# Tie order of a top-k selection and the place of the sample rows' retention, in a one-layer hybrid decoder step

## The chip, the cores and the metric

One core of a Trainium2 chip runs the whole kernel as one program. The metric is the device time of one execution in microseconds; lower is better. Times of several executions are compared by their median.

## What is computed

One decoder layer for a prompt of 1024 tokens and for 8 sample rows with a past of 2048 tokens each, on shared weights:

```python
x = LN1(alpha*x + 0.5*SwiGLU_1(x))
h = x @ w_in                      # q,k,v of attention; indexer q,k,w; q,k,v,gate of retention
# attention, 8 heads x 64: an indexer scores all causal keys,
I[t,s] = sum_h w[t,h] * relu(q_idx[t,h] . k_idx[s])
# lax.top_k keeps 256 keys per query (ties: the lowest index first); softmax over those with a bias
# retention, 4 heads x 128: per chunk, o = (q k^T * decay) v + (q S) * decay ; S = g*S + k^T v
#   sample rows: one step, S_new = gamma_h * S + k v^T ; o = q S_new ; group norm, swish gate
x = LN2(alpha*x + concat(A, R) @ w_out)
x = LN3(alpha*x + 0.5*SwiGLU_2(x))
```

The outputs are y for prompt and samples, the new k, v and indexer-key rows, and the retention states. The 8 sample states are 4 x 128 x 128 floats each (256 KB), read and written once.

## The kernel before

**Layout.** Activations lie transposed, in three column chunks of 344 tokens (`CW`, together 1032). A projection tile of 128 output columns is three calls of `dense` (line 169 to 171: 24 matmuls of 128x344 into one PSUM bank of kind `mm`), followed by an evacuation per chunk (`ev`) on ScalarE and VectorE. PSUM has 8 banks; in the stage in question (`MB`, line 1947) they are `mm=[0,1]`, `sc=[3,4]`, `po=[2,5]`, `aux=[6,7]`; each kind rotates over its banks, so the third chunk of a run of tiles waits until the first one's bank is evacuated.

**The planner.** The work is written as Python generators driven by `Sched`. Each generator emits some instructions and yields a delay in planner microseconds; the main line emits a half tile of matmuls and ticks the planner clock by 1.75, and due generators emit between. `drain` and `until` tick by 0.25 until a generator has ended or a condition holds. So the planner fixes the program order. The framework then orders each engine's own queue at build time, mostly in program order, but it lets a later instruction pass one that it expects to be held up. On the chip each queue runs strictly in its order.

**The stage in question.** In program order after the gate tile of the last retention head:

- `topk` (line 1010) has searched each query row's 256th largest score bit by bit. Its tail (lines 1063 to 1079) settles ties: for each key block b it counts scores at or over the threshold (`ge`, line 1068), marks equal ones (`eq`, 1069), scans them (`pf`, 1070), works out how many to drop (`need`, 1072 and 1073), and builds the mask `M[b]` (1075 and 1076 on VectorE, 1077 on ScalarE). Block b has (b+1)*128 columns. The order is b = 2 to 7, with yields of 2.5 and 2.0. `done.add(b)` lets the attention use that block.
- `ret_core(3)` finishes the last prompt retention head (matmuls `rs`, `ro`, `pyt`; VectorE lines 1156 to 1215).
- `sret` (line 1221) does the sample rows' retention: it loads two states, then per sample b broadcasts the value row on TensorE (`spread`, line 1100, into an `sc` bank), scales the state on ScalarE (1254, four instructions), multiplies and adds on VectorE (1255, 1256), stores the state from the SP queue (1258), multiplies it with q into a `po` bank that is kept for all eight samples (1260, eight instructions), and loads the state for b+2 (1263). A norm, four transposes (1277) and a store of 16 KB (1281) end it. Its yields per sample are `sr_step` = 3.0 and 1.0. It is started right behind the last gate tile.
- The main line emits the tiles va0, qa0, ka0 (attention values, queries and keys of head pair 0), drains `topk` between qa0 and ka0, and then starts `att_lane`, which runs 8 units per head pair: logits into `sc`, mask and bias on VectorE, exponential on ScalarE, transposes into `aux`, products with the values into a `po` bank. `g.po_free` counts free `po` banks. The units of the first three pairs begin with the largest query blocks (6 and 7).
- Under pair 0's attention it emits va1 and qa1 with a pace of 2.0, drains `sret`, and goes on with ka1. So it goes on to pair 3, the output projection and the second SwiGLU.

Of the kernel before, what the change touches and what calls it, by code (L numbers as in the profile page):

```python
# [15 lines left out]
F32 = mybir.dt.float32  # L16
# [10 lines left out]
P = 128  # L27
D = 1024
NTOK = 1032
CW = 344  # L30
# [55 lines left out]
def bank(g, kind, name):  # L86

    ks = g.banks[kind]
    t = g.ps.tile([P, 512], F32, tag=f"b{ks[g.bi[kind] % len(ks)]}", name=name, bufs=1)
    g.bi[kind] += 1  # L90
    return t
# [6 lines left out]
def A(g, slot, name, dt=F32, n=NTOK):  # L98

    return g.ap.tile([P, n], dt, tag=f"a{slot}", name=name, bufs=1)  # L100
# [909 lines left out]
def topk(g, S, M, tk, hi, lo, scr, tie, done):  # L1010


    nc = g.nc
    V = nc.vector
    bl = ACTB + DVEB
    na = len(ACTB)
    lim, cn = tk['c'][:, 0:6], tk['c'][:, 6:12]
    cnt, t, t2, c, lim2, T1 = (tk[k] for k in ('cnt', 't', 't2', 'cond', 'lim2', 'T1'))
    for j, b in enumerate(bl):
        n = (b + 1) * 128  # L1020
        sortkey(g, S[b], n, scr[0], scr[1], hi[b], lo[b])
        yield 2.5
    g.keysdone = True
    key = hi
    for ph in range(2):
        V.memset(t, -0.5 if ph == 0 else 32767.5)
        L = lim if ph == 0 else lim2

        def count(nm):
            for j, b in enumerate(bl):  # L1030
                n = (b + 1) * 128
                if j < na:
                    jk = g.ms.tile([P, 1024], BF, tag="ja", name=f"ja{nm}{b}", bufs=1)
                    nc.scalar.activation(jk[:, 0:n], key[b], AF.Sign, bias=t[:, j:j + 1], scale=-1.0, accum_out=cnt[:, j:j + 1])  # L1034
                else:
                    jk = g.ms.tile([P, 640], BF, tag="jv", name=f"jv{nm}{b}", bufs=1)
                    V.tensor_scalar(out=jk[:, 0:n], in0=key[b], scalar1=t[:, j:j + 1], scalar2=None, op0=OP.is_lt, op1=OP.add, accum_out=cnt[:, j:j + 1])

        count(f"{ph}x")
        for bit in range(15, -1, -1):  # L1040
            step = 2.0 ** bit
            nc.gpsimd.tensor_scalar(out=t2, in0=t, scalar1=0.5 * step, scalar2=None, op0=OP.subtract)
            yield g.tk_step
            V.tensor_tensor(out=c, in0=cnt, in1=L, op=OP.is_le)
            V.scalar_tensor_tensor(out=t, in0=c, scalar=step, in1=t2, op0=OP.mult, op1=OP.add)  # L1045
            if bit:
                count(f"{ph}_{bit}")

        if ph == 0:
            V.tensor_copy(T1, t)  # L1050
            V.tensor_scalar(out=t, in0=t, scalar1=0.5, scalar2=None, op0=OP.add)
            count("g")
            for j, b in enumerate(bl):
                V.scalar_tensor_tensor(out=lo[b], in0=hi[b], scalar=T1[:, j:j + 1], in1=lo[b], op0=OP.is_equal, op1=OP.mult)
                if j % 2:
                    yield 2.0
            V.tensor_tensor(out=lim2, in0=lim, in1=cn, op=OP.add)
            V.tensor_tensor(out=lim2, in0=lim2, in1=cnt, op=OP.subtract)
            key = lo
    th = tk['th']  # L1060
    threshold_bits(g, T1, t, tk['i0'], tk['i1'], th)
    ge, eq, pf = tie()
    for b in (2, 3, 4, 5, 6, 7):
        j = bl.index(b)
        n = (b + 1) * 128
        thj = th.bitcast(F32)[:, j:j + 1]
        need = g.ms.tile([P, 1], F32, tag="need", name=f"need{b}", bufs=2)
        V.tensor_scalar(out=ge[:, 0:n], in0=S[b], scalar1=thj, scalar2=None, op0=OP.is_ge, op1=OP.add, accum_out=cnt[:, j:j + 1])
        V.tensor_scalar(out=eq[:, 0:n], in0=S[b], scalar1=thj, scalar2=None, op0=OP.is_equal)
        V.tensor_tensor_scan(out=pf[:, 0:n], data0=eq[:, 0:n], data1=eq[:, 0:n], initial=0.0, op0=OP.add, op1=OP.bypass)  # L1070

        V.tensor_scalar(out=need, in0=cnt[:, j:j + 1], scalar1=-1.0, scalar2=256.0, op0=OP.mult, op1=OP.add)
        V.tensor_tensor(out=need, in0=need, in1=pf[:, n - 1:n], op=OP.add)
        yield 2.5
        V.scalar_tensor_tensor(out=eq[:, 0:n], in0=pf[:, 0:n], scalar=need, in1=eq[:, 0:n], op0=OP.is_gt, op1=OP.mult)
        V.tensor_tensor(out=ge[:, 0:n], in0=ge[:, 0:n], in1=eq[:, 0:n], op=OP.subtract)
        nc.scalar.activation(M[b], ge[:, 0:n], AF.Identity, bias=g.nbig[:, 0:1], scale=BIG)
        done.add(b)
        yield 2.0


class Rows:
# [135 lines left out]
    nc.sync.dma_start(mscr[hd, :, 0:1024], gT[:, 0:1024])  # L1218


def sret(g, smp, state_ret, state_out, mscr, sa, sb):

    nc = g.nc
    V = nc.vector
# [2 lines left out]
    ks = cv(32).rearrange("p (h b) -> p h b", h=4)  # L1227
    qm = cv(256).rearrange("p (h b) -> p h b", h=4)
    kv = cv(512).rearrange("p (h v) -> p h v", h=4)
    vn = Rows(g, [g.ms.tile([40, CW], F32R, tag="silu", name=f"srr{j}", bufs=2)[:, 0:256] for j in range(2)])  # L1230
    mix = cv(32).rearrange("p (h b) -> p h b", h=4)
    st = cv(24, rows=8).rearrange("p (h b) -> p h b", h=4)
    mv = cv(8, rows=8).rearrange("p (h b) -> p h b", h=4)
# [8 lines left out]
    for b in range(2):  # L1242
        nc.sync.dma_start(s2[b], state_ret[b].rearrange("h d v -> d h v"))
    yield 3.0
    while not g.po_free:
        yield 0.5
    g.po_free -= 1
    po = bank(g, 'po', "sro")
    for b in range(8):
        s0 = s2[b % 2]  # L1250
        pv = bank(g, 'sc', f"srv{b}")
# [13 lines left out]
    o = s2[0][0:8]  # L1265
    nc.scalar.copy(o, po[0:8].rearrange("p (h v) -> p h v", h=4))
    g.po_free += 1
    for h in range(4):
        V.bn_stats(out=st[:, h, :], in_=o[:, h, :])
        V.bn_aggr(out=mv[:, h, :], in_=st[:, h, :])  # L1270
# [679 lines left out]
def trunk(tc, i, o):  # L1950
# [156 lines left out]
    for c in range(NCH):  # L2107
# [3 lines left out]
        if c == 2:  # L2111
            S_.close("msL")
            zt = [X(g, f"z{q}", f"zt{q}") for q in range(3)]
            M, S = {}, {}
            mt = zt[0][:, 0:2304].bitcast(BF)
            for b in range(8):
                M[b] = mt[:, b * (b + 1) // 2 * 128:(b + 1) * (b + 2) // 2 * 128]
            cz = Carve(zt[0], 8 * CW)
            cz(2304)
            sbias = cz(128).rearrange("p (c h) -> p c h", c=16)  # L2120
            for k in ('qaT', 'kaT', 'vaT', 'q', 'k', 'g', 'v'):
                smp[k] = cz(32).rearrange("p (a b) -> p a b", a=4)
            g.kvd = cz(4)
            g.wsmp = cz(8, rows=8)
            g.ptab = cz(1, I32)
            sel = dict(np64=cz(2, rows=64), row=cz(16, I32), bkt=cz(16, I32), bias=sbias, rel_bias=i['rel_bias'])
            cz = Carve(zt[1], 8 * CW)
            for b in (7, 6, 5):
                S[b] = cz((b + 1) * 128)
            cz = Carve(zt[2], 8 * CW)  # L2130
            for b in (4, 3, 2):
                S[b] = cz((b + 1) * 128)
            sx = cz(130)[:, 0:129]
            _, g.coff, _ = pack()
            g.csts = cz(i['csts'].shape[1])
            g.qis = cz(32).rearrange("p (a b) -> p a b", a=4)
            g.stats = [(cz(48).rearrange("p (a b) -> p a b", a=8), cz(16).rearrange("p (a b) -> p a b", a=8), cz(8)) for _ in range(2)]
            tk = dict(c=cz(12))
            for k in ('cnt', 't', 't2', 'cond', 'lim2', 'T1'):
                tk[k] = cz(6)  # L2140
            for k in ('i0', 'i1', 'th'):
                tk[k] = cz(6, I32)
            nc.sync.dma_start(g.csts, i['csts'])
            nc.sync.dma_start(tk['c'], i['tkc'])
            nc.sync.dma_start(g.kvd, i['kvd'])
            g.ms = S_("msI")
            cm = g.ms.tile([P, 256], F32, name="cmask")
            nc.sync.dma_start(cm, i['cmask'])
            g.cmask = cm[:, 0:128]
            nc.vector.tensor_copy(M[0], cm[:, 128:256])  # L2150
            nc.vector.memset(M[1][:, 0:128], 0.0)
            nc.vector.tensor_copy(M[1][:, 128:256], cm[:, 128:256])
# [81 lines left out]
    g.tk_step, g.s2_step, g.s3_step = 3.2, 2.5, (4.0, 2.0)  # L2234

    def tie_tiles():
        t = A(g, 16, "tie").bitcast(BF)
        return t[:, 0:1024], t[:, 1024:2048], A(g, 17, "tief")

    tks = s.add(topk(g, S, M, tk, hi, lo, (u, sk), tie_tiles, g.mdone))  # L2240
    sm = Carve(g.ms.tile([P, 988], F32, tag="s1", name="s1sm", bufs=1), 988)
# [1 line left out]
    for hd in (1, 2, 3):  # L2243
# [8 lines left out]
        t = A(g, 6, f"gT{hd}")  # L2252
        tile(ev_copy(g, t, smp['g'][:, hd, :], AF.Silu), f"gr{hd}")
        gT[hd] = t
    sr = s.add(sret(g, smp, i['state_ret'][0], o['ret_state_sample'][0], mscr, A(g, 20, "sra"), A(g, 21, "srb")))


    kout = o['k_prompt'][0, 0].rearrange("t h d -> t (h d)")
# [19 lines left out]
    s.drain(*cores)  # L2278
    nat = s.add(after())
    tile(pair_q(g, 0, pr[0], smp, A(g, 9, "q00", F32R, 1024), A(g, 1, "q10", F32R, 1024))[0], "qa0")  # L2280
    s.drain(tks, nat)
    g.z2 = zt[2]
    nat = s.add(keys(0, g.z2[:, 0:1024], 0.0)())
    s.drain(nat)
    S_.close("msR")
    g.ms = S_("msA")
    g.nt_tag = "nt"
    qz = X(g, "z1", "qx", F32R)
    qx = qz[:, 0:2048]
    g.low = [(0, g.ms.tile([P, 512], F32R, name="klA")), (320, qz[:, 2048:2752])]  # L2290
    pr[0].ready = True
    lane = s.add(att_lane(g, pr, M, ascr))
    s.tick(0)
    for ct in (1, 2, 3):
        s.drain(nat)
        after = values(ct, g.z2[:, 0:1024], g.att_pace)
        s.until(lambda: ct == 1 or pr[ct - 2].done())
        nat = s.add(after())
# [265 lines left out]
```

## Time and profile before

| | us |
|---|---|
| median of 3 runs | 2315.74 |
| lowest and highest of them | 2314.35 and 2316.15 |
| the profiled execution's own time | 2317.26 |
| its span in the trace | 2315.5 |
| TensorE busy | 2223.6 |
| VectorE busy | 1760.2 |
| ScalarE busy | 1071.5 |

The span covers all but 1.8 us of the profiled execution's time. Busy times are sums over the span and hide where an engine waits; the stage in question lies at 1106 to 1215 us.

### The profile page before, as it was taken

How to read it: one execution, taken by the hardware profiler on the slowest of the kernel's cores; microseconds unless marked ns; L12 is line 12 of the kernel's file. 1: busy time of each engine (PE TensorE's matmuls, PEld its weight loads, DVE VectorE, ACT ScalarE, POOL GpSimd, SP SyncE). 2: the span in 40 equal slices, each digit the busy share in tenths (PEclk: the TensorE clock that was granted, in tenths of full speed). 3: DMA queues.
4: the chain of work that ended last, by engine and by line, in shares of the span. 5: the costliest groups of instructions: out<-in, count | busy, mean ns of one | idle time of the engine just before them, and what ended most of it. 6: DMA issues, size and time to landing. Idle time of an engine off the chain costs nothing.

```text
span 2315.5 us, 36887 instructions
## 1 busy us (share of the span) xinstructions
PE 2223.6 (96%) x14155; PEld 2147.5 (93%) x14155; DVE 1760.2 (76%) x3745; ACT 1071.5 (46%) x1931; POOL 326.1 (14%) x342
## 2 busy tenths in 40 slices
PE   8999999999999999899899999889999999999996
PEld 8999999999999998888789889879799999999996
DVE  5755797887878588777966678988468789887876
ACT  5433343342434466887456664353445444343331
POOL 0000100000002303454023224313210000000002
PEclk9999999999999999999899999989999999999998
DMA  8544332222222201222222142436544332222311
GB/s 266 153 138 146 108 90 74 83 76 64 82 78 96 92 23 46 57 74 58 85 72 56 44 148 71 130 119 191 168 136 137 93 109 80 92 73 64 92 65 49
DMA packets 239182, 224.32 MB, mean 97 GB/s; under 512 B 13098, under 2 KB 219774, under 8 KB 238238
## 3 DMA queue, kind: packets, MB, share of 16 engines
q1 hardware_dynamic: 235166, 209.38, 29.9%
q0 software_dynamic: 3840, 12.59, 1.7%
q8 instruction: 111, 1.82, 0.3%
q14 instruction: 65, 0.53, 0.1%
HBM read 200.91 MB, written 22.59 MB: 97 GB/s over the span
## 4 chain that ended last, share of the span: by engine, by line
PE 76%; DVE 11%; ACT 7%; issue 3%; DMA 2%; POOL 1%; SPq 0%; POOLq 0%; DVEq 0%; ACTq 0%
PE pds_f L403 5%; PE pds_f L404 5%; PE pds_f L405 5%; ACT ja L1034 3%; PE pg_f L169 2%; PE pg_f L170 2%; PE pu_f L169 2%; PE pdp_f L403 2%; PE pg_f L171 2%; PE pdp_f L404 2%; PE pdp_f L405 2%; PE pu_f L171 2%; PE pu_f L170 2%; PE ps_f1U L169 2%; PE ps_f2G L170 2%
## 5 line engine op out<-in xcount | busy, mean ns | idle before, releaser
L407 DVE SCALAR_TENSOR_TENSOR z<-pds_f,z 128x344 f32<-128x344 f32 x320 | 164.7, 516 | 126.4 <-PE pds_f L405 125.1
L403 PE MATMUL pds_f<-gs_f,wh_f1ds 128*128 128x344 f32 x352 | 114.3, 325 | 0.1
L407 DVE SCALAR_TENSOR_TENSOR z<-pdp_f,z 128x344 f32<-128x344 f32 x160 | 80.0, 512 | 44.1 <-PE pdp_f L405 43.9
L405 PE MATMUL pds_f<-gs_f,wl_f1ds 128*128 128x344 f32 x352 | 113.5, 322 | 0.0
L403 PE MATMUL pds_f<-gs_f,wh_f2ds 128*128 128x344 f32 x352 | 113.4, 322 | 0.0
L404 PE MATMUL pds_f<-gs_f,wh_f1ds 128*128 128x344 f32 x352 | 113.4, 322 | 0.0
L405 PE MATMUL pds_f<-gs_f,wl_f2ds 128*128 128x344 f32 x352 | 112.4, 319 | 0.0
L404 PE MATMUL pds_f<-gs_f,wh_f2ds 128*128 128x344 f32 x352 | 112.4, 319 | 0.0
L1034 ACT ACTIVATE ja<-key,zt 128x1024 bf16<-128x1024 int16 (+5 forms) x90 | 93.8, 1042 | 37.3 <-DVE zt L1045 30.2
L723 POOL TENSOR_TENSOR yt<-yt,ln_b_rows 128x512 f32<-128x512 f32 (+1 forms) x9 | 12.0, 1351 | 570.3 <-ACT yt L722 570.3
L296 ACT CAST wS_f1G<-ws_f1G 128x512 fp32r<-128x512 f32 x44 | 25.0, 618 | 133.4 <-PE pds_f L404 68.1
L1508 ACT CAST p<-pT 128x512 fp32r<-128x512 f32 (+2 forms) x112 | 47.5, 434 | 54.2 <-PE pT L1504 42.0
L296 ACT CAST wS_f2G<-ws_f2G 128x512 fp32r<-128x512 f32 x44 | 25.7, 619 | 93.4 <-PE pds_f L405 80.7
L403 PEld LDWEIGHTS pds_f<-gs_f,wh_f1ds 128*128 128x128 f32 x352 | 66.9, 190 | 1.0 <-DVE z L407 0.3
L404 PEld LDWEIGHTS pds_f<-gs_f,wh_f1ds 128*128 128x128 f32 x352 | 67.0, 190 | 0.2
L405 PEld LDWEIGHTS pds_f<-gs_f,wl_f1ds 128*128 128x128 f32 x352 | 66.8, 190 | 0.0
L403 PEld LDWEIGHTS pds_f<-gs_f,wh_f2ds 128*128 128x128 f32 x352 | 66.2, 188 | 0.2 <-ACT gs_f L465 0.2
L404 PEld LDWEIGHTS pds_f<-gs_f,wh_f2ds 128*128 128x128 f32 x352 | 66.2, 188 | 0.0
L405 PEld LDWEIGHTS pds_f<-gs_f,wl_f2ds 128*128 128x128 f32 x352 | 66.1, 188 | 0.0
L612 POOL TENSOR_TENSOR lns_l<-z 128x344 f32<-128x344 f32 x3 | 2.8, 938 | 442.2 <-DVE z L407 428.0
L1509 DVE TENSOR_TENSOR p<-pT,p 128x512 fp32r<-128x512 f32 (+2 forms) x112 | 54.5, 497 | 8.7 <-ACT p L1508 7.5
L169 PE MATMUL pg_f<-xh,wh_f1g 128*128 128x344 f32 x176 | 57.5, 326 | 2.8 <-ACT xh L762 2.8
(815 smaller groups left out, 8651.8 us busy)
## 6 DMA issues: line engine op xcount, KB each, us to landing
wr_f1g<-in_ffn_wg_dram SPq DMA_DIRECT2D x22, 512.0 KB
wr_f1u<-in_ffn_wu_dram SPq DMA_DIRECT2D x22, 512.0 KB
wr_f1dp<-in_ffn_wd_dram SPq DMA_DIRECT2D x22, 512.0 KB
wr_f1G<-in_ffn_wg_dram SPq DMA_DIRECT2D x22, 512.0 KB
wr_f1U<-in_ffn_wu_dram SPq DMA_DIRECT2D x22, 512.0 KB
wr_f1ds<-in_ffn_wd_dram SPq DMA_DIRECT2D x22, 512.0 KB
wr_f2u<-in_ffn_wu_dram SPq DMA_DIRECT2D x22, 512.0 KB
wr_f2g<-in_ffn_wg_dram SPq DMA_DIRECT2D x22, 512.0 KB
```

The lines of the kernel that those rows point to most:

```text
L169: g.nc.tensor.matmul(ps, w[0][:, k, :], x[0][:, k, :], start=first and i == 0, stop=False)
L170: g.nc.tensor.matmul(ps, w[0][:, k, :], x[1][:, k, :], start=False, stop=False)
L171: g.nc.tensor.matmul(ps, w[1][:, k, :], x[0][:, k, :], start=False, stop=last and i == n - 1)
L296: nc.scalar.copy(t[:, 0], src)
L403: g.nc.tensor.matmul(ps, wh[:, o, :], th, start=i == 0, stop=False)
L404: g.nc.tensor.matmul(ps, wh[:, o, :], tl, start=False, stop=False)
L405: g.nc.tensor.matmul(ps, wl[:, o, :], th, start=False, stop=i == len(grp) - 1)
L407: g.nc.vector.scalar_tensor_tensor(out=z, in0=ps, scalar=0.5 / ALPHA, in1=z, op0=OP.mult, op1=OP.add)
L723: nc.gpsimd.tensor_tensor(out=y[0:n, sl], in0=y[0:n, sl], in1=gb['ln3_b'][0:n, sl], op=OP.add)
L1034: nc.scalar.activation(jk[:, 0:n], key[b], AF.Sign, bias=t[:, j:j + 1], scale=-1.0, accum_out=cnt[:, j:j + 1])
L1508: nc.scalar.copy(ph[:, js, ts], ptv[:, js, ts])
L1509: nc.vector.tensor_tensor(out=pl[:, js, ts], in0=ptv[:, js, ts], in1=ph[:, js, ts].bitcast(F32), op=OP.subtract)
```

## The change

It reverses the order in which ties are settled (b = 7 first), and lets the generator yield 3.0 and 3.5 instead of 2.5 and 2.0. The tie tiles lie in slots 14 and 15 instead of 16 and 17, `need` lies in a long-lived tile. The main line waits before ka0 only until blocks 6 and 7 are settled, and for the rest of `topk` at the start of pair 1's tiles. ka0's transposed keys lie in `zt[1]` instead of `zt[2]`. `sret` starts when `topk` and `ret_core(3)` have ended; it takes bank 5 for its sum, leaves bank 2 as the only `po` bank until that sum is read, and has one row tile of 512 columns instead of two of 256.

```diff
-    for b in (2, 3, 4, 5, 6, 7):
+    for b in (7, 6, 5, 4, 3, 2):
...
-        need = g.ms.tile([P, 1], F32, tag="need", name=f"need{b}", bufs=2)
+        need = tk['need'][:, b % 2:b % 2 + 1]
...
-        yield 2.5
+        yield 3.0
...
-        yield 2.0
+        yield 3.5
...
-def sret(g, smp, state_ret, state_out, mscr, sa, sb):
+def sret(g, smp, state_ret, state_out, mscr, sa, sb, rows):
...
-    vn = Rows(g, [g.ms.tile([40, CW], F32R, tag="silu", name=f"srr{j}", bufs=2)[:, 0:256] for j in range(2)])
+    vn = Rows(g, [rows])
...
-    while not g.po_free:
-        yield 0.5
-    g.po_free -= 1
-    po = bank(g, 'po', "sro")
+    while g.po_free < 2:
+        yield 0.25
+    g.po_free = 1
+    g.banks['sr'], g.bi['sr'], g.banks['po'] = [5], 0, [2]
+    po = bank(g, 'sr', "sro")
...
     g.po_free += 1
+    g.banks['po'] = [2, 5]
...
+            tk['need'] = cz(2)
...
-        t = A(g, 16, "tie").bitcast(BF)
-        return t[:, 0:1024], t[:, 1024:2048], A(g, 17, "tief")
+        t = A(g, 14, "tie").bitcast(BF)
+        return t[:, 0:1024], t[:, 1024:2048], A(g, 15, "tief")
...
-    sr = s.add(sret(g, smp, i['state_ret'][0], o['ret_state_sample'][0], mscr, A(g, 20, "sra"), A(g, 21, "srb")))
+    sr = s.add(later(lambda: not s.live(tks) and not any(s.live(e) for e in cores), lambda: sret(
+        g, smp, i['state_ret'][0], o['ret_state_sample'][0], mscr, A(g, 20, "sra"), A(g, 21, "srb"), A(g, 7, "srr", F32R)[0:40, 0:512])))
...
-    s.drain(tks, nat)
+    s.drain(nat)
+    s.until(lambda: {6, 7} <= g.mdone)
     g.z2 = zt[2]
-    nat = s.add(keys(0, g.z2[:, 0:1024], 0.0)())
+    nat = s.add(keys(0, zt[1][:, 0:1024], 0.0)())
...
-    qz = X(g, "z1", "qx", F32R)
-    qx = qz[:, 0:2048]
-    g.low = [(0, g.ms.tile([P, 512], F32R, name="klA")), (320, qz[:, 2048:2752])]
...
         s.drain(nat)
+        if ct == 1:
+            s.drain(tks)
+            qz = X(g, "z1", "qx", F32R)
+            qx = qz[:, 0:2048]
+            g.low = [(0, g.ms.tile([P, 512], F32R, name="klA")), (320, qz[:, 2048:2752])]
```

## Rows read from the trace of the kernel before

**Rows 1.** The page, part 1: busy us (share of the span) xinstructions.
```profile
PE 2223.6 (96%) x14155; PEld 2147.5 (93%) x14155; DVE 1760.2 (76%) x3745; ACT 1071.5 (46%) x1931; POOL 326.1 (14%) x342
```

**Rows 2.** Busy time by stretch: va0 to ka0, then va1 and qa1.
```profile
core 0: us, PE busy (x) PEld busy (x) DVE busy (x) ACT busy (x) POOL busy (x), PEclk, DMA share, GB/s
1105.85:1179.22 73.37, 63.04 (x365) 55.22 (x365) 62.86 (x138) 29.59 (x74) 8.92 (x5) 0.88 0.32 91
...
1179.22:1214.99 35.77, 33.59 (x220) 31.61 (x219) 22.06 (x80) 18.82 (x43) 8.62 (x11) 1.00 0.26 68
```

**Rows 3.** Timeline of TensorE: start us, us, instruction, count, idle before and its releaser.
```profile
1118.16 0.76 PE L1100 MATMUL srv<-srr,sel 40*128 40x256 f32 x2 [3.64 <-DVE need L1072]
...
1134.81 0.79 PE L1100 MATMUL srv<-srr,sel 40*128 40x256 f32 x2 [2.93 <-DVE srb L1255]
...
1161.05 0.39 PE L169 MATMUL pw_ka<-h1h,wh_ka 128*128 128x344 f32 x1 [3.76 <-DVE q L1418]
```

**Rows 4.** Timeline of TensorE: a projection matmul behind the first wait, one behind the third.
```profile
1119.30 0.49 PE L170 MATMUL pw_va<-h1l,wh_va 128*128 128x344 f32 x1
...
1161.28 0.32 PE L170 MATMUL pw_ka<-h1l,wh_ka 128*128 128x344 f32 x1
```

**Rows 5.** Timeline of VectorE: the instructions that ended the three waits, and one scan.
```profile
1117.75 0.26 DVE L1181 SCALAR_TENSOR_TENSOR kd<-kd,rs 128x128 f32<-128x128 f32 x1
...
1134.07 0.68 DVE L1255 TENSOR_TENSOR srb<-srv,srb 128x512 f32<-128x512 f32 x1
...
1155.20 2.28 DVE L1070 TENSOR_TENSOR_SCAN tief<-tie 128x1024 f32<-128x1024 bf16 x1
...
1160.39 0.52 DVE L1418 SCALAR_TENSOR_TENSOR q<-pw_qa,q 64x344 fp32r<-64x344 f32 x1
```

**Rows 6.** Groups of VectorE, 1105.85 to 1179.22: xcount | busy us, mean ns | idle before.
```profile
L1070 DVE TENSOR_TENSOR_SCAN tief<-tie 128x384 f32<-128x384 bf16 (+5 forms) x6 | 9.7, 1620 | 0.1
L1075 DVE SCALAR_TENSOR_TENSOR tie<-tief,need,tie 128x384 bf16<-128x384 f32 (+5 forms) x6 | 5.7, 950 | 0.1
L1255 DVE TENSOR_TENSOR srb<-srv,srb 128x512 f32<-128x512 f32 x8 | 5.5, 685 | 0.1
L1256 DVE TENSOR_TENSOR sra<-sra,srb 128x512 f32<-128x512 f32 x8 | 5.5, 683 | 0.1
...
L1403 DVE TENSOR_TENSOR kk<-pw_ka,k 64x344 fp32r<-64x344 f32 x4 | 2.1, 519 | 2.0 <-ACT k L1400 1.9
...
L1215 DVE SCALAR_TENSOR_TENSOR gT<-pyt,prm,gT 128x512 f32<-128x512 f32 x2 | 1.5, 752 | 2.2 <-PE pyt L1212 2.2
...
L1096 DVE TENSOR_TENSOR srr<-srvn,srr 8x256 fp32r<-8x256 f32 x2 | 0.8, 414 | 0.1
```

**Rows 7.** Timeline of TensorE: one sample's product, and one sample's broadcast.
```profile
1127.11 1.04 PE L1260 MATMUL sro<-sra,srb 128*8 128x128 f32 x8
...
1143.73 0.50 PE L1100 MATMUL srv<-srr,sel 40*128 40x256 f32 x2
```

**Rows 8.** Groups of ScalarE, 1105.85 to 1179.22: the scaling of the states.
```profile
L1254 ACT ACTIVATE sra<-sra 128x128 f32<-128x128 f32 x25 | 5.7, 300 | 0.6 <-DMA sra<-in_state_ret_dram 0.5
```

**Rows 9.** Waits of the SP queue, 1100 to 1220: us in total, times, longest us.
```profile
SPq L1258 <- DVE sra L1256: 20.7, 6, 9.7
...
SPq L142 <- POOL wl_ka L154: 6.2, 2, 5.5
...
SPq L1531 <- DMA out_k_prompt_dram<-knn: 2.4, 1, 2.4
```

**Rows 10.** Timeline of SP's issues: the last state store, pair 0's bias, the last store.
```profile
1177.43 0.37 SPq L1258 DMA_DIRECT2D ut_ret_state_sample_dram<-sra  x1
...
1189.32 0.81 SPq L1531 DMA_DIRECT2D T<-scr  x2
1190.23 0.39 SPq L1281 DMA_DIRECT2D mscr<-srb  x1
```

**Rows 11.** The tile in slot 15 ahead of the ties: first and last start.
```profile
L1600 ACT COPY kts<-pks x16: 565/580/587, 946.9 to 1048.4; 128x512 f32<-128x512 f32 x16
```

## The prediction, on record before the changed kernel ran

> **What bounds the kernel now.** I read the page's busy shares first, then busy times by stretch, then TensorE's timeline for its gaps, and last VectorE's groups in the same stretch. TensorE is busy 96% of the span [rows 1], so in most stretches work that moves costs nothing and gains nothing; only a gap in TensorE's line, or matmuls at a lower clock, can be won. The stretch from va0 to ka0 is such a place: of 73.37 us TensorE is busy 63.04, at a mean granted clock of 0.88, while VectorE is busy 62.86 [rows 2]. The 10.33 us of idle time are three waits, 3.64 + 2.93 + 3.76, all on VectorE [rows 3]. What VectorE was late with: the last `kd` step, which frees the `sc` bank that the first sample's broadcast takes; the product that frees the bank of a later broadcast; and qa0's second evacuation, which frees ka0's first bank [rows 5]. Each stood in a queue of ties: a scan alone takes 2.28 us for block 7 [rows 5]. After the first wait a projection matmul takes 0.49 us against 0.32 [rows 4]: the lower of the two clock levels, 1.2 instead of 2.4 GHz. With 0.88 granted, 12% of the 63.04 us, 7.6 us, is what the lower level cost. So 10.3 + 7.6 = 17.9 us is the most that this stretch can give. In the next one, va1 and qa1, TensorE is idle only 35.77 - 33.59 = 2.2 us, at a clock of 1.00, and VectorE has 13.7 us free [rows 2].
>
> **The change part by part.**
>
> *Retention of the sample rows leaves va0 to ka0.* TensorE loses there 8 samples x (1.04 + 0.50) = 12.3 us [rows 7]; it pays them again beside va1 and qa1, so on TensorE itself this is worth nothing. VectorE loses 5.5 + 5.5 + 0.8 = 11.8 us [rows 6], and that is the gain, since VectorE is late here. At full clock TensorE's own work left is 63.04 - 7.6 - 12.3 = 43.1 us. VectorE's is 62.86 - 11.8 = 51.1 us, plus the 2.2 us that it waits for the `pyt` transposes [rows 6], 53.3 us. It still exceeds TensorE's 43.1, so VectorE sets the length: 53.3 us. Gain: 73.4 - 12.3 - 53.3 = 7.8 us. What is late next is the evacuation of qa0: its first bank must be free for the third chunk, and ties of 7, 6 and 5 stand before it. The ends for this term: 43.1 us if the ties of 5 to 2 slip behind the evacuations and cover nothing (gain 18.0), and no gain if TensorE waits as long for qa0's banks as it waited at the three places. I take 53.3, since the queue is strict and the ties come earlier in program order.
>
> *Order of ties, wider steps, the shorter wait before ka0.* The same six sets of instructions run, so nothing is added or removed. Their yields sum to 6 x 6.5 = 39 planner us instead of 27, which puts VectorE's pieces further apart and lets evacuations between. The drain before ka0 holds back no matmul by itself, as ties have none on TensorE; what it changes is whose instructions come first. Blocks 7 and 6 suffice for the first unit. I cost it at nothing beyond the sum above.
>
> *Slots, `need`, `zt[1]`, one row tile.* Slot 15's last use ends at 1048.4 [rows 11], 60 us before a tie, so the move costs nothing. The block-7 scores under ka0's keys in `zt[1]` are dead once tie 7 has run, which is first. One broadcast of 512 columns instead of two of 256: between 0 and 0.25 us per sample, half a 0.50 us pair [rows 7]; I take 0.
>
> *Retention beside va1 and qa1.* TensorE there gets 33.59 + 12.3 = 45.9 us, VectorE 22.06 + 11.8 = 33.9, ScalarE 18.82 + 32 x 0.30 = 28.4 [rows 2, 8]: TensorE stays the bound and covers both. On the SP queue go two plus six loads, eight stores of 256 KB and the 16 KB store. The stores waited 20.7 us in all for VectorE's sums, and the first weight load behind such waits and the split of the last one 6.2 [rows 9]. None showed as a wait of TensorE. New is that the bias of pair 0 (two loads, 1189.32) and the weights of qa1 and ka1 queue behind those stores; before, all eight stores were out by 1177.43 [rows 10]. POOL makes the row tile and the masks for attention; it is busy 8.62 of 35.77 us [rows 2].
>
> *The new waits.* `sret` waits for two free `po` banks. By the planner the ties (39) end before ka0's output transposes do: half of va0, the rest of head 3, qa0, ka0 and those transposes come to some 45, an estimate from the yields. Then it takes bank 5 before the first unit asks. Attention then has one `po` bank for some 50 us; a unit's product phase lasts 10 to 15 planner us and the first begins 20 after the lane, so only the second unit waits. `drain(sr)` before ka1 now holds ka1, its output transposes and pair 1's lane. For these waits the trace has no row. The ends: below nothing, -2.2 us if the added matmuls fill the idle time of that stretch [rows 2]; above, +15.6 us (third rival). I take +1, near the lower end, since VectorE has room there.
>
> **Sum.** 7.8 - 1.0 = 6.8 us off the profiled execution's 2317.26 is 2310.5. That execution is 1.5 over the median of 2315.74, so I predict 2309.0.
>
> **A rule against my clock term.** The trace shows 0.88 granted in this stretch and 1.00 in the next [rows 2]. The Trainium skill, "TensorE: Matmul & The Clock Gate", section "What's actually happening", says that for modelling the ramp penalty is under 1% of a typical span and should not be fitted. By it the most to be won would be the 10.3 us of waits, and 2305.4 the best time. The 7.6 us are 0.3% of this span, so page and row don't conflict; but that is the size of the effect here, and I keep the row.
>
> **The rivals.**
>
> *All of it is won.* The three waits and the lower clock go, and the ties of 5 to 2 hide under the attention's start. For it: no wait of the three is on the ties' own results. Against: 51.1 us of VectorE stand against 43.1 of TensorE. Time: 2317.3 - 18.0 - 1.5 = 2297.8.
>
> *The wait moves.* The largest ties now come first, so at qa0's evacuation VectorE has 21 of the 33 column blocks behind it, instead of 18 (blocks 2 to 5) plus four samples' products. If TensorE stands there for about 10 us, at the lower clock after, nothing is won: 2313 to 2318. For it: scans and drops are 9.7 + 5.7 us, and the evacuations wait behind them in the queue [rows 6]. Against: va0's evacuations are on ScalarE alone, so TensorE has va0 and two chunks of qa0 to run before it needs VectorE. Also here: a change that does less than it says, as queues are reordered at build time.
>
> *Slower: ka1 is held by the samples.* From the first broadcast at 1118.16 [rows 3] to the last store at 1177.43 and the end at 1190.23 [rows 10] `sret` took 72 us. If it takes as long beside attention, it ends some 24 us after the 48 us that va1 and qa1 then need (45.9 + 2.2). In those only attention feeds TensorE: of 33.59 us, 21 are six chunks of 3.5 planner us, so attention is 12.6 of 35.77, 35%. 24 x 0.65 = 15.6 us idle, less 7.8 won: 7.8 slower, 2323.5. It decides from a hold of 12 us on. For it: one `po` bank, two `sc` banks shared with the logits, stores on one strict queue. Against: the 72 us were spent behind a VectorE that was busy 86% [rows 2], and the planner spaces samples by 4 us plus 1.5 of matmuls, 44 in all.
>
> **How the numbers follow.** Forecast (2303 to 2312): 0.47. All won (2297 to 2303): 0.15. The wait moves: 0.25. Slower: 0.13. A measurement of this kernel can tell about 0.2%, 4.6 us, from no change: 2311.1 to 2320.4 is no difference. Faster by more: 0.15 plus nearly all of the first, 0.62; within: 0.25; slower: 0.13. The range of 2299 to 2321 leaves out the best part of "all won" (about 0.07) and most of the slow case (0.11).
>
> **What would show it.** Right: the waits of 3.64, 2.93 and 3.76 us are gone; va1 starts about 53 us after va0; VectorE is busy over 90% between; the granted clock is over 0.95; the samples' products lie between va1 and ka1, which starts 46 to 50 us after va1. Wrong: a wait of several us at qa0's third chunk or at ka0 for line 1417 or 1418; a gap before ka1 that ends with the row tile or the sum of `sret`; waits of attention for bank 2; or a later stretch that gives the time back.

## The result: 0.7% slower, and the profile after

| | before | after |
|---|---|---|
| median, us (4 runs each, beside one another) | 2315.94 | 2332.01 |
| lowest and highest | 2314.35 and 2316.71 | 2330.45 and 2334.52 |
| span of the profiled execution | 2315.5 | 2328.7 |

The ratio is 1.0069, with an interval of 1.0057 to 1.0081: 16 us slower where 7 us faster was predicted, and outside the range of 2299 to 2321. TensorE's busy time grew by 6.9 us and its idle time by 6.3 (page, part 1 of the changed kernel, against [rows 1]):

```profile
PE 2230.5 (96%) x14147; PEld 2149.2 (92%) x14147; DVE 1762.3 (76%) x3744; ACT 1071.8 (46%) x1930; POOL 329.9 (14%) x341
```

Three stretches of the changed kernel, then all from va2's first matmul to just behind the output projection (busy time by stretch, columns as in [rows 2]):

```profile
core 0: us, PE busy (x) PEld busy (x) DVE busy (x) ACT busy (x) POOL busy (x), PEclk, DMA share, GB/s
1105.73:1161.70 55.97, 44.81 (x279) 43.52 (x278) 50.35 (x120) 21.59 (x45) 8.03 (x4) 0.91 0.19 54
1161.70:1209.32 47.62, 45.94 (x289) 37.84 (x287) 26.77 (x75) 27.30 (x72) 12.52 (x15) 1.00 0.40 113
1209.32:1256.91 47.59, 43.85 (x262) 37.40 (x262) 34.79 (x123) 26.70 (x66) 11.14 (x15) 0.89 0.16 43
1256.91:1533.74 276.83, 257.51 (x1710) 239.85 (x1710) 212.34 (x718) 144.06 (x312) 86.34 (x99) 0.99 0.31 95
```

va0 to va1 takes 55.97 us where it took 73.37 [rows 2], va1 to ka1 47.62 where it took 35.77: at ka1 the changed kernel is 5.7 us ahead (1209.32 against 1214.99). Then ka1 to va2 takes 47.59 us. Before, the same stretch and the one behind it read:

```profile
1214.99:1231.41 16.42, 16.42 (x118) 16.31 (x117) 11.04 (x31) 11.03 (x24) 4.97 (x6) 1.00 0.16 41
1231.41:1517.90 286.49, 269.92 (x1837) 252.94 (x1835) 223.11 (x770) 160.27 (x355) 91.63 (x111) 0.99 0.31 92
```

So 31.2 us go between ka1 and va2, and at va2 the changed kernel is 25.5 us behind. Not all of that is lost: in the long stretch, attention, which ran ahead meanwhile, leaves TensorE less to do. It hands back 9.7 us of it; 15.8 remain behind the output projection, and 13.2 at the end.

Timeline of the changed kernel around that place (three engines in order of time):

```profile
1220.99 0.50 PE L1100 MATMUL srv<-srr,sel 40*128 40x512 f32 x1
...
1224.02 1.04 PE L1261 MATMUL sro<-sra,srb 128*8 128x128 f32 x8
...
1225.10 0.58 ACT L1267 COPY sra<-sro 8x512 f32<-8x512 f32 x1 [0.15 <-PE sro L1261]
...
1229.56 0.32 PE L171 MATMUL pw_ka<-h1h,wl_ka 128*128 128x344 f32 x1
...
1231.06 1.10 DVE L1275 TENSOR_SCALAR sra<-sra,srb 8x128 f32<-8x128 f32 x4
...
1233.13 0.22 PE L1279 MATMUL srpt<-ident,sra 8*128 8x8 f32 x1
...
1233.39 1.34 ACT L1402 CAST k<-pw_ka 64x344 fp32r<-64x344 f32 x3 [1.09 <-PE srpt L1279]
...
1244.66 0.49 PE L169 MATMUL pw_ka<-h1h,wh_ka 128*128 128x344 f32 x1
```

Eight samples now run beside attention, the last broadcast at 1220.99 and the last product at 1224.02, and the norm and the four transposes follow, the last at 1233.13. ka1's first casts into its key tiles (line 1402) start on ScalarE right behind the last of them and name it as their releaser. ka1's keys go to slots 20 and 21, which are the slots of `sra` and `srb`; until the samples have read these for the last time, ka1's first bank can't be emptied. Its matmuls stop at 1229.56, with two chunks done, and go on at 1244.66. I call this **the hold**.

Its longer part lies behind the samples. Four casts and six subtractions empty a chunk's bank, and they stand among attention's steps in the queues of ScalarE and VectorE: here the last subtraction comes 10.9 us after the last transpose has ended, while before the whole evacuation of that chunk took 4.9 us. The first and the last subtraction of the changed kernel, then the first copy and the last subtraction before:

```profile
1240.60 1.02 DVE L1405 TENSOR_TENSOR kl<-pw_ka,k 64x344 fp32r<-64x344 f32 x2
...
1243.88 0.38 DVE L1405 TENSOR_TENSOR qx<-pw_ka,k 64x24 fp32r<-64x24 f32 x2
```
```profile
1219.64 0.45 ACT L1396 COPY zt<-pw_ka 128x344 f32<-128x344 f32 x1 [1.45 <-PE pw_ka L171]
...
1224.15 0.38 DVE L1403 TENSOR_TENSOR qx<-pw_ka,k 64x24 fp32r<-64x24 f32 x2
```

The stretch ka1 to va2 of the changed kernel, cut at the two ends of the hold:

```profile
1209.32:1229.56 20.24, 20.11 (x137) 17.14 (x137) 14.96 (x57) 10.87 (x28) 6.48 (x8) 1.00 0.25 72
1229.56:1244.66 15.10, 12.01 (x60) 8.98 (x59) 12.42 (x49) 9.73 (x24) 3.23 (x6) 0.86 0.12 28
1244.66:1256.91 12.25, 11.72 (x68) 11.27 (x68) 7.40 (x19) 6.10 (x14) 1.43 (x1) 0.76 0.05 13
```

In the hold TensorE isn't idle for 15 us, only for 3.1: attention fills it. After it, ka1's third chunk runs at a granted clock of 0.76.

In the stretch va0 to va1, the three waits of [rows 3] are gone and one of 8.18 us has come, at the transposes `pyt` of the last prompt head. Timeline of the changed kernel, VectorE and then TensorE:

```profile
1132.43 1.49 DVE L1070 TENSOR_TENSOR_SCAN tief<-tie 128x640 f32<-128x640 bf16 x1
...
1134.09 0.88 DVE L1068 TENSOR_SCALAR_CACHE_REDUCE tie<-zt 128x640 bf16<-128x640 f32 x1
...
1137.43 0.51 DVE L1419 SCALAR_TENSOR_TENSOR q<-pw_qa,q 64x344 fp32r<-64x344 f32 x1
...
1139.56 1.22 DVE L1070 TENSOR_TENSOR_SCAN tief<-tie 128x512 f32<-128x512 bf16 x1
1140.69 2.11 DVE L1203 TENSOR_SCALAR o<-o,zt 128x128 f32<-128x128 f32 x8
...
1141.07 0.47 PE L1212 MATMUL pyt<-ident,o 128*128 128x128 f32 x1 [8.18 <-DVE o L1203]
```

What `pyt` waits for is line 1203's `o`, and ahead of it VectorE's queue holds a chain of small steps of the norm with ties (a scan of 1.49, a count of 0.88, another scan of 1.22) and qa0's evacuations between them. Before the change the samples' matmuls stood there; in the kernel with the ties changed and the samples early (the first experiment below) TensorE's longest waits from va0 to va1 are 4.18, 2.44 and 1.09 us, and none is at `pyt`.

### The profile page after: what moved, and what is told of

Same layout as the page of the kernel before. It is cut to its first block, busy times and chain, and to the rows that moved or that the text cites. A ratio compares the mean times of both kernels' runs of the same rounds, so it can differ in the third digit from the quotient of the medians.

```text
span 2328.7 us, 36844 instructions
## 1 busy us (share of the span) xinstructions
PE 2230.5 (96%) x14147; PEld 2149.2 (92%) x14147; DVE 1762.3 (76%) x3744; ACT 1071.8 (46%) x1930; POOL 329.9 (14%) x341
## 5 line engine op out<-in xcount | busy, mean ns | idle before, releaser
L1510 ACT CAST p<-pT 128x512 fp32r<-128x512 f32 (+2 forms) x112 | 47.6, 432 | 51.9 <-PE pT L1506 37.2
```

The costliest lines, as they stand in the source:

```text
L1510: nc.scalar.copy(ph[:, js, ts], ptv[:, js, ts])
```

## The experiments

All are timed against the kernel before on the same chip (10 or 11 runs each; 5 in the one named). Medians of before lay between 2315.9 and 2316.5 throughout, so a difference of two kernels timed on different chips carries some 0.6 us of doubt from that alone. The theory at the start: the hold is the cost. The rivals: one bank for attention's products; the order of the ties; the samples' work beside attention as such.

**Ties only.** The changed kernel, with the samples started at once, as before.

```diff
-    sr = s.add(later(lambda: not s.live(tks) and ..., lambda: sret(...)))
+    sr = s.add(sret(...))
```

> The changed kernel, but the samples' retention starts right behind the last gate tile, as before. Theory hold (ka1's keys wait until the retention has let go of slots 20 and 21, which costs the time): the hold is gone, since the retention ends before va1; ka1 to va2 takes about 16 us as before and the time is 2308 to 2318. Theory ties (blocks 7 and 6 first put a long VectorE queue before qa0 and that wait of 8 us is what is lost): the wait stays and the time is 2326 or more. Theory bank (attention with one po bank is what is lost): as theory hold, since the bank is back before attention starts; this run does not part those two.

2312.92 us, ratio 0.9988 (0.9978 to 0.9997). A second time, with the three kernels below that build on it:

> The kernel of 2312.9 us once more, for a narrower interval on the same chip as the three above: 2311 to 2315, ratio 0.998 to 0.9995 to the kernel before.

2313.69 us, ratio 0.9986 (0.9977 to 0.9995). So without the samples' later start the change gains 2.5 to 3 us, and this version is faster than before, if by little. The time and the missing hold are as theory hold had them; theory bank had them too. Its windows (va0 to va1, va1 to ka1, ka1 to va2) have no hold:

```profile
1105.00:1172.69 67.69, 58.47 (x358) 50.12 (x356) 62.18 (x137) 29.71 (x73) 8.96 (x5) 0.95 0.34 98
1172.69:1208.77 36.08, 34.97 (x220) 32.83 (x219) 22.36 (x80) 18.60 (x42) 8.49 (x11) 0.95 0.27 69
1208.77:1225.19 16.42, 16.42 (x119) 16.31 (x117) 11.05 (x31) 11.02 (x24) 4.93 (x6) 1.00 0.16 41
```

**The wider steps in it.** The same with yields of 2.5 and 2.0.

```diff
-        yield 3.0
+        yield 2.5
...
-        yield 3.5
+        yield 2.0
```

> The kernel of 2312.9 us with the ties' yields of 2.5 and 2.0 as before instead of 3.0 and 3.5, so that what is left of the change is the order, the slots, one row tile and the shorter wait ahead of ka0. If the wider steps help there, as they let evacuations between: 2315 to 2318. If they only make the ties end later: 2310 to 2313.

2313.50 us, ratio 0.9989 (0.9980 to 0.9998): no difference from 2313.69. The steps gain nothing. **The order alone**, put into the kernel before with the wider steps:

```diff
-    for b in (2, 3, 4, 5, 6, 7):
+    for b in (7, 6, 5, 4, 3, 2):
```

> The kernel before, with nothing but the order of ties (7 first) and their wider steps. Theory hold: nothing depends on the order of ties but where VectorE is late between va0 and ka0; 2311 to 2320, and no more than 5 us from before. Theory ties: 2322 or more, with a TensorE wait of 6 to 9 us at the transposes of the last prompt retention head. Theory bank: 2311 to 2320.

2320.61 us, ratio 1.0022 (1.0013 to 1.0032). The order with wider steps costs 4.7 us as long as the main line waits for all ties before ka0: just outside theory hold's range, and below theory ties'. In its trace 2.3 us are won from va0 to va1 (71.05 us) and 6.7 lost from va1 to ka1 (42.43 instead of 35.77). The gain in the version above therefore needs something besides the order and the steps. The shorter wait, for blocks 6 and 7 alone, is the likely part; that version differs from this one also in the slots, `need` and the row tile, and no run parts these.

**Samples only.** The changed kernel with order, yields and wait of the ties as before.

```diff
-    for b in (7, 6, 5, 4, 3, 2):
+    for b in (2, 3, 4, 5, 6, 7):
...
-    s.drain(nat)
-    s.until(lambda: {6, 7} <= g.mdone)
+    s.drain(tks, nat)
```

> The changed kernel with the ties as before (2 first, steps 2.5 and 2.0) and all of them drained before ka0: only the samples' retention is moved. Theory hold: the hold of ka1 is there, 25 to 30 us from ka1's first matmul to va2 beyond the 16 of before; 2324 to 2336. Theory ties: 2310 to 2320. Theory bank: 2324 to 2336, as the bank is taken too.

2320.76 us, ratio 1.0023 (1.0013 to 1.0033), with 28.0 us from ka1 to va2. A miss for all three: the hold is there, but 11.6 us beyond 16.4 instead of 25 to 30, and the time lies between the ranges. **Old steps in the changed kernel** (the edit of the steps above):

> The changed kernel with the ties' steps at 2.5 and 2.0 again, 7 first. The ties end 12 planner us earlier and with them the retention starts 8 to 12 us earlier. Theory hold: ka1 to va2 falls from 47.6 to 34 to 40 us and the time to 2320 to 2326. Theory bank: 2325 to 2330. If the wider steps were what frees VectorE's queue at qa0: 2332 or more.

2320.39 us, ratio 1.0015 (1.0006 to 1.0025), ka1 to va2 30.5 us. The time is in theory hold's range, the stretch shorter than expected. The wider steps end the ties later, so the samples start later and the hold is longer: 11.6 us of the changed kernel's time hang on them. The halves don't add up: -2.5 and +4.9 alone, +16 together.

**One bank.** The kernel before, with bank 2 alone for attention's products from the lane's start to ka1.

```diff
+    g.po_free, g.banks['po'] = 1, [2]
     pr[0].ready = True
...
+        if ct == 1:
+            g.po_free, g.banks['po'], g.bi['po'] = g.po_free + 1, [2, 5], 1
```

> The kernel before, with its samples' retention where it was, but attention has bank 2 alone from its start to ka1, as in the change. This measures the disputed cost by itself. Theory hold: the second unit waits a little and nothing else, 2314 to 2319. Theory bank: 2322 to 2332.

2318.08 us, ratio 1.0005 (0.9995 to 1.0015): nothing that can be told. But the run has the single bank for less of attention's products than the change does. Its first product comes 5 us before ka1 (1210.84), where the bank goes back; in the changed kernel the products begin at 1190.27, and the samples' sum is read at 1225.10, 35 us on. The first product of this run, and of the changed kernel:

```profile
1205.71 0.28 PE L1490 MATMUL po<-p,v 128*128 128x256 f32 x1
```
```profile
1190.27 0.28 PE L1492 MATMUL po<-p,v 128*128 128x256 f32 x1
```

What one bank costs for 35 us without a hold is not tested.

**Samples quicker**, and **samples earlier** (start when the last prompt head has ended, whatever the ties do), then both.

```diff
-        yield 1.0
+        yield 0.25
...
-    yield 4.0
+    yield 1.5
...
-    g.sr_step = 3.0
+    g.sr_step = 1.0
```
```diff
-    sr = s.add(later(lambda: not s.live(tks) and not any(
+    sr = s.add(later(lambda: not any(
```

> The changed kernel with the retention's planner steps cut from 3.0, 1.0 and 4.0 to 1.0, 0.25 and 1.5, so that it ends sooner; order of ties, place and bank as in the change. Theory hold: its last read of slot 20 comes 15 to 25 us earlier than the 1233 us of the changed kernel, the gap in ka1 shrinks by as much, and the time falls to 2314 to 2324. Theory ties: unchanged, 2329 to 2335. Theory bank: falls too, by the share of the bank's time that is saved, some 4 to 8 us: 2324 to 2328.

2321.40 us, ratio 1.0022 (1.0013 to 1.0032), ka1 to va2 32.3 us: in theory hold's range, though the last transpose comes only 7.4 us earlier, at 1225.77.

> The changed kernel, but the samples' retention starts when the last prompt retention head has ended, while ties 5 to 2 still run. Theory hold: it starts some 20 us earlier, so the last read of slot 20 comes near 1212, about where ka1 starts; from ka1 to va2 20 to 28 us instead of 47.6; time 2314 to 2322. Theory bank: attention has one bank for the shorter rest, 2322 to 2328. Neither (the order of ties together with any later place loses the time): 2329 or more.

2322.94 us, ratio 1.0027 (1.0017 to 1.0037), ka1 to va2 18.2 us. The hold is all but gone and 6.5 us of loss stay, just above what theory hold allowed and inside theory bank's range. 5 of them lie before ka1 (1220.20, where before had 1214.99). The two longest waits there, in its timeline of TensorE, are `pyt` and the samples' own transposes:

```profile
1140.79 0.47 PE L1212 MATMUL pyt<-ident,o 128*128 128x128 f32 x1 [9.74 <-DVE o L1203]
...
1197.70 0.24 PE L1279 MATMUL srpt<-ident,sra 8*128 8x8 f32 x1 [3.04 <-DVE sra L1275]
```

> Both: the start of e5_samples_at_qa0 and the shorter steps of e4_samples_quick. Theory hold: the retention ends before ka1's first evacuation needs slots 20 and 21, the hold is gone (ka1 to va2 16 to 20 us), the waits between va0 and ka0 are as in the change or a little longer; 2309 to 2317. Theory bank: 2314 to 2322.

2316.66 us, ratio 1.0004 (0.9994 to 1.0013), ka1 to va2 16.4 us. Both together lose nothing, and gain nothing; the time is in both theories' ranges.

**The hold by itself.** To have a hold without samples beside attention, I took the version of 2313.69 us, where they run early, and let only their four last transposes wait until 17 planner us behind the drain ahead of ka1, and in a second kernel 8.

```diff
     yield 4.0
+    while g.hold is None or g.s.t < g.hold + 17.0:
+        yield 0.5
     pt = bank4(g, 'aux', "srpt")
...
+            g.hold = s.t
             s.drain(sr)
```

> As the kernel of 2312.9 us (ties changed, samples early), but the four transposes that end the samples' retention, and with them the release of slots 20 and 21, wait until 17 planner us behind the drain ahead of ka1, about where the changed kernel has them. No sample's product, store or broadcast lies beside attention. If the hold of the slots is what costs: the stretch from ka1 to va2 grows from 16.4 to 40 to 50 us, attention's matmuls lose 10 to 15 us to waits and the lower clock, and the time is 2323 to 2330. If the samples' own work beside attention is what costs: 2311 to 2316.

2319.33 us, ratio 1.0012 (1.0003 to 1.0021), ka1 to va2 41.7 us.

> The same with 8 planner us instead of 17. If the hold costs in proportion to its length beyond some point: ka1 to va2 is 24 to 32 us and the time 2315 to 2321, between the two others. If only the samples' work costs: 2311 to 2316, as with 17.

2321.39 us, ratio 1.0018 (1.0009 to 1.0027), ka1 to va2 29.2 us. A hold without samples beside attention costs 5.6 and 7.7 us: real, but less than half of the 18 us between 2313.7 and 2332.0, and the shorter one isn't cheaper. Two runs for the rest:

**Early samples and the hold together**: the kernel of 2322.94 us with the wait of 17.

> The samples start when the last prompt head has ended (2322.9 us) and their four closing transposes wait until 17 planner us behind the drain ahead of ka1 (which cost 5.6 us where the samples start early). If the two costs add up: ka1 to va2 of 35 to 45 us and a time of 2326 to 2331, near the changed kernel's 2332.0. If they are one cost seen twice, since attention gets ahead in either: 2321 to 2325.

2318.03 us, ratio 1.0009 (1.0000 to 1.0018), ka1 to va2 37.2 us. Neither expectation: with a hold added, the kernel is 4.9 us *faster*. So a hold is no plain sum of lost time.

**The small ties later**: blocks 5 to 2 wait until the last prompt head has ended.

```diff
+        while b < 6 and not g.cd:
+            yield 0.5
...
     s.drain(*cores)
+    g.cd = True
```

> The kernel of 2322.9 us with the ties of blocks 5 to 2 waiting until the last prompt head has ended, so that VectorE's products for that head do not queue behind them. If the wait of 9.7 us in front of the retention's transposes is what the later start costs: the wait shrinks below 4 us and the time falls to 2314 to 2319. If VectorE's work only moves and the wait comes back at qa0's or ka0's evacuations: 2320 to 2325.

2321.58 us, ratio 1.0025 (1.0016 to 1.0034). The wait at `pyt` is as long as without the edit:

```profile
1141.32 0.48 PE L1214 MATMUL pyt<-ident,o 128*128 128x128 f32 x1 [9.76 <-DVE o L1205]
```

VectorE's queue came out in the same order, scans of blocks 4 and 3 ahead of `o` and all, so this run doesn't test the price of that wait, though the time fell into the second range; it stays open.

**The bank in a hold.** The kernel of 2318.03 us with bank 5 handed back behind the hold (5 runs); and the changed kernel with the samples' sum in bank 7, so that attention keeps both banks for products.

```diff
-    g.po_free += 1
-    g.banks['po'] = [2, 5]
     for h in range(4):
...
+    g.po_free += 1
+    g.banks['po'] = [2, 5]
     pt = bank4(g, 'aux', "srpt")
```
```diff
-    while g.po_free < 2:
-        yield 0.25
-    g.po_free = 1
-    g.banks['sr'], g.bi['sr'], g.banks['po'] = [5], 0, [2]
+    g.banks['sr'], g.bi['sr'], g.banks['aux'] = [7], 0, [6]
...
-    g.po_free += 1
-    g.banks['po'] = [2, 5]
+    g.banks['aux'] = [6, 7]
```

> As the run of 2318.0 us (samples from qa0 on, their last transposes 17 planner us behind the drain), but bank 5 goes back to attention behind that hold instead of ahead of it. If one bank during the hold is what the changed kernel pays for: fewer products by qa2 (92 or less instead of 100) and 2325 to 2333. If a bank is worth as little in the hold as without it: 2317 to 2321.

2324.53 us, ratio 1.0035 (1.0022 to 1.0049), ka1 to va2 31.2 us, and 92 products by qa2: the first expectation, but for half a microsecond. One bank in this hold costs 6.5 us.

> The changed kernel with the samples' sum in bank 7 instead of 5, so that attention keeps both its banks for products and has one instead of two for its transposes until the sum is read. If the bank of the products is what costs: 2318 to 2325. If the samples' late work beside attention is: 2329 to 2334. One bank for the transposes may cost something of its own, which would show as waits of the transposes.

2319.99 us, ratio 1.0016 (1.0006 to 1.0025): 12.0 us back from one edit, as the first theory had it, while ka1 to va2 is nearly as long as in the changed kernel. No transposes wait for long: TensorE idles for 0.7 us in front of them from 1160 to 1260. Busy time of this run from ka1 to va2, and from there to just behind the output projection:

```profile
1215.46:1258.31 42.85, 40.14 (x249) 33.46 (x247) 32.94 (x118) 23.98 (x60) 9.56 (x13) 0.92 0.17 44
1258.31:1524.65 266.34, 253.34 (x1711) 236.15 (x1710) 205.95 (x716) 145.18 (x315) 86.59 (x99) 1.00 0.32 99
```

Compare the last row with that of the changed kernel: 266.34 us against 276.83 for the same tiles. Up to va2 the bank is worth nothing (1258.31 against 1256.91, with 80 products done in either), and 10.5 us behind it: TensorE is idle for 13.0 instead of 19.3 us there, and busy 4.2 us less.

**Where it comes back, and where not.** In the timelines of TensorE I counted attention's products with the values (320 in all) up to qa2, up to ka3 and up to the output projection's first matmul. The two right columns compare the profiled executions with before. Each is one execution; that of samples only lies 3.6 us below the median of its kernel, that of quick samples 4.3 us above.

| kernel | ka1 to va2 | ka3 at | products by qa2 | by ka3 | by the output projection | ka3 later by | ka3 to the end, longer by |
|---|---|---|---|---|---|---|---|
| before | 16.4 | 1350.1 | 65 | 172 | 192 | | |
| ties only, again | 16.4 | 1347.6 | 65 | 172 | 192 | -2.5 | +0.1 |
| samples at qa0, no hold | 18.2 | 1354.3 | 77 | 172 | 184 | +4.2 | +2.4 |
| samples only | 28.0 | 1350.1 | 80 | 172 | 192 | 0.0 | -0.1 |
| old steps | 30.5 | 1354.3 | 84 | 180 | 200 | +4.2 | -1.0 |
| quick samples | 32.3 | 1356.2 | 96 | 180 | 192 | +6.1 | +2.3 |
| changed kernel | 47.6 | 1364.6 | 92 | 184 | 201 | +14.5 | -1.3 |
| hold of 8 | 29.2 | 1356.2 | 92 | 184 | 201 | +6.1 | -1.7 |
| hold of 17, one bank | 31.2 | 1360.7 | 92 | 184 | 201 | +10.6 | -1.6 |
| hold of 17 | 41.7 | 1359.6 | 100 | 184 | 211 | +9.5 | -7.4 |
| hold of 17, samples at qa0 | 37.2 | 1361.6 | 100 | 184 | 211 | +11.5 | -10.0 |
| changed kernel, two banks | 42.9 | 1365.0 | 100 | 184 | 211 | +14.9 | -10.1 |

What a product of lead is worth can be estimated from two rows above: by va2 the variant with two banks has done 80 products where before has done 32, and from there on TensorE is busy 253.34 us instead of 269.92, some 0.35 us for each. The 12 products of lead at ka3 are then worth some 4 us. In the last three kernels 7.4 to 10.1 us come back behind ka3, in the three ahead of them 1.3 to 1.7. Both groups have that lead; what parts them is mostly idle time. Behind va2 TensorE idles for 13.0 us in the variant with two banks, and for 18.6 and 18.8 in the hold of 8 and in the hold of 17 with one bank:

```profile
1240.35:1524.19 283.84, 265.29 (x1768) 246.22 (x1766) 218.59 (x739) 150.66 (x328) 88.63 (x101) 0.99 0.31 93
```
```profile
1248.58:1528.98 280.40, 261.61 (x1753) 243.34 (x1753) 217.47 (x731) 148.54 (x323) 87.79 (x99) 0.99 0.31 94
```

What goes with it is how far attention is when qa2 starts: 92 products in the one group, 100 in the other, and 201 or 211 by the output projection. In two pairs of these kernels the difference is attention's bank, and there it moves the count from 92 to 100; but the hold of 8 has both banks and 92 as well. I call this **the alignment** of attention's units with the tiles. The changed kernel and its variant with two banks are within half a microsecond at ka3, and 8.4 apart at the end. The mark of it in the trace is VectorE's wait for ScalarE in the units' product phase. Groups of VectorE from va2 on, of the changed kernel, of its variant with two banks, of the hold of 8 and of before:

```profile
L1511 DVE TENSOR_TENSOR p<-pT,p 128x512 fp32r<-128x512 f32 (+2 forms) x84 | 41.2, 496 | 17.3 <-ACT p L1510 16.5
```
```profile
L1507 DVE TENSOR_TENSOR p<-pT,p 128x512 fp32r<-128x512 f32 (+2 forms) x84 | 41.3, 496 | 10.1 <-ACT p L1506 9.4
```
```profile
L1513 DVE TENSOR_TENSOR p<-pT,p 128x512 fp32r<-128x512 f32 (+2 forms) x92 | 44.9, 494 | 18.9 <-ACT p L1512 18.0
```
```profile
L1509 DVE TENSOR_TENSOR p<-pT,p 128x512 fp32r<-128x512 f32 (+2 forms) x102 | 49.1, 491 | 8.0 <-ACT p L1508 7.0
```

Per instruction that is 206, 120, 205 and 78 ns of waiting (203 in the hold of 17 with one bank; 125 and 123 in the other two holds of 17). I read it as units that overlap less, with fewer instructions of another unit between; that isn't shown, nor why a given hold leaves them so.

## Why the prediction was wrong

**The stretch va0 to ka0: right, a little too high.** Predicted 53.3 us from va0 to va1, with VectorE busy over 90% of it and a clock over 0.95; measured 55.97, 50.35 of VectorE (90%), and 0.91. The gain was 73.37 - 12.3 - 55.97 = 5.1 us instead of 7.8. The step "what is late next is the evacuation of qa0" named the wrong place: `pyt` came first, with 8.18 us. The kernel with the samples early has no such wait, so it is the samples' leaving that let it show. The second rival, "the wait moves", had the mechanism, but at another place; of its time, 2313 to 2318, the kernels with the samples taken away and no hold are one in (2316.7, quick samples) and two out (2322.9 and 2321.6).

**Retention beside va1 and qa1: right in the number, in part by luck.** "46 to 50 us", measured 47.62; TensorE busy 45.94, predicted 45.9. But the sum put all eight samples there; only six of them multiplied before ka1, and somewhat more of attention's matmuls than before filled the rest. At ka1 the kernel was 5.7 us ahead, where the sum said 6.8.

**"The new waits ... I take +1, near the lower end": this step failed.** From ka1 to the end the changed kernel lost 5.7 + 13.2 = 18.9 us. The step took the planner's spacing for the samples' end, 44 us in all; on the chip the first broadcast came at 1167.95 and the last transpose at 1233.13, 65 us on and 24 behind ka1's start. And it took `drain(sr)` for a wait of the program order. What held ka1's bank was the slot: 20 and 21 are pair 1's keys, and the casts into them waited for the last reader of `sra`. The program order alone did not stop ka1: its matmuls start 24 us ahead of the last transpose. Behind the transposes its evacuation then took another 10.9 us. The diff shows both numbers, and nowhere did the prediction ask who has slots 20, 21 and 7 next. It did so for slot 15, because there the change moved the tile; here it moved the *time*, with the same effect.

**The third rival: the mechanism was right, its price was not.** "ka1 is held by the samples" has the samples end 24 us late, as they did, and TensorE idle for 65% of that. But from ka1 to va2 it idled for 3.7 of 47.59 us, and the clock of 0.89 took 11% of the busy 43.85, another 4.8; attention filled the rest. The loss shows behind it: attention ran ahead, and the delay wasn't made up. By the table it is 14.5 us of delay at ka3, less 1.3 after it; the kernel with two banks, with the same delay, has 10.1 back. The hold by itself (same edits but for it) costs 5.6 to 7.7. Of the 18.3 us between the ties-only kernel and the changed one, 6.3 come with the late samples while attention keeps both banks (2319.99 against 2313.69), and 12.0 with the single bank, which goes with the alignment; in another hold the bank cost 6.5. These are medians from different chips, and the alignment's own cause stays open.

**"Attention then has one `po` bank ... so only the second unit waits": its price was wrong.** In the changed kernel 12.0 us hang on that bank, and its trace shows them behind va2, not as waits in the hold. The run without a hold, where one bank costs nothing that can be told (1.0005), has it beside only the first products.

**The clock.** The 7.6 us of [rows 2] were worth counting, but little of the loss is clock. From va0 to va1 the lower level took 9% of 44.81 us, 4.0 instead of 7.6, and from ka1 to va2 it took 4.8 that were not there before: 1.2 us more in all. The mean granted clock of the whole span is 0.983 before and 0.981 after, idle time included. The Trainium skill, "TensorE: Matmul & The Clock Gate", section "What's actually happening", puts the ramp penalty at under 1% of a typical kernel span. Here the whole span's clock lies 1.7% and 1.9% below full; in TensorE's busy time alone, by the trace's clock records, 27.8 and 29.6 us go to the lower level, 1.2% and 1.3%. So the trace shows somewhat more than the page's figure, and a difference of only 1.8 us.

Not tried: state tiles in slots that ka1 doesn't use, which would take the hold away and leave the samples late, and would also part the slot's share from that of `drain(sr)`, during which attention's units are emitted ahead of ka1. The kernel of 2316.66 us comes nearest: samples beside attention, but ended before ka1.

## What to carry to other kernels

When work is moved later, look up who takes over each of its buffers, and by when; a slot's next owner is a due time that the planner doesn't know. A stall that other work fills isn't free: the delay must be made up later, and in this case that hung on how far attention had come, by a cause that stays open. Parts of a change don't add up: here the ties' part gained 2.5 us, the samples' part cost 4.9, and together they cost 16; the late samples cost 6 us with two banks for attention and 18 with one.

## What the runs showed that was not expected

Adding a hold made a kernel faster (2322.94 to 2318.03 us; against before on their own chips, 6.5 us slower became 2.0 slower): 37.2 us from ka1 to va2 instead of 18.2, and afterwards 266.14 us to the end of the output projection, at a granted clock of 1.00 in both rows. The windows of that run:

```profile
1218.21:1255.38 37.17, 35.85 (x242) 31.01 (x241) 29.74 (x101) 24.36 (x60) 10.34 (x16) 1.00 0.13 32
1255.38:1521.52 266.14, 253.28 (x1712) 236.07 (x1710) 206.28 (x716) 144.86 (x315) 86.56 (x99) 1.00 0.33 99
```

The lower clock level outlasts the gaps that it came with. In the changed kernel TensorE was busy 20.11 of 20.24 us, then 12.01 of 15.10 at 0.86, and then 11.72 of 12.25 at 0.76. A hold need not bring it: the one of 37.2 us above ran at 1.00 from ka1 to va2, that of 41.7 us (the hold of 17) at 0.92:

```profile
1211.35:1253.08 41.73, 38.59 (x246) 33.62 (x244) 30.64 (x102) 25.48 (x63) 10.86 (x18) 0.92 0.13 30
```
